# The delta-rule recurrence of a two-layer encoder on whole 128x128 tiles, with its loads spread out and its mixes in pairs

## The chip, the cores and the metric

The kernel runs on one core of one Trainium2 chip. A core has TensorE (PE in the profile, with PEld for its loads of weights), VectorE (DVE), ScalarE (ACT), GpSimd (POOL) and SyncE (SP), which here issues the DMAs. The metric is the device time of one execution in microseconds; before the change it is 2475.38 us, the median of 3 runs (2474.15 to 2476.15).

## The reference, cut to what matters

A trunk of two layers on a stream of 256 frames by 2048 channels, in float32. The first layer is an RWKV-7 time mixing with an MLP behind it; the second is an attention with forget gates and an MLP. The change touches the first layer's time mixing:

```
h  = rms_norm(x) ; prev = h shifted by one frame
xs = h + (prev - h) * x_mix[n]              # six mixes: r, k, v, w, a, g
r, k, v = xs[0..2] @ w_rkv[0..2]            # 2048 x 2048 each
decay, a, g from small two-step products of xs[3..5]
# per head (32 heads of 64), frame by frame, state S (64 x 64):
S_t = S_{t-1} diag(decay_t) + (S_{t-1} a_t) b_t^T + v_t k_t^T ;  y_t = S_t r_t
out = (group_norm(y) + bonus) * g @ w_o
```

## The kernel before

**Layout.** The 2048 channels are 16 slices of 128 partitions; a slice holds two heads of 64 channels, head 0 on partitions 0 to 63 and head 1 on 64 to 127 (`HA`, `HB`). A unit `u` is two slices, so four heads; there are 8 units. Frames are cut into 4 chunks of 64 (`NCH`). Inside a chunk the recurrence is solved with matrices: the lower-triangular system of a chunk is inverted (`inv`), then a chain over the 4 chunks carries the state (`rec`).

**Big products.** The weights stay in DRAM. `load_split` (L193 to 208) loads a raw piece `wr`, ACT casts it to a rounded fp32r copy `wh` (L203) and DVE takes the rest `wl` (L205). A few casts go to DVE (every `share["h"]`-th) and a few rests to POOL (every `share["l"]`-th). Each product is then three: wh with the high and the low part of the moving operand, wl with the high part (L211 to 213; L767 to 769 for v).

**Streams and plans.** The first layer is written as generators, one per piece of work, each yielding after a small step: `h` (norm and shifted difference), `mk`/`mr`/`mv` (the mixes for k, r, v, split into the operands opB, opA, opB), `lw`/`la`/`lg` (first small products), `gk`/`gr`/`gv` (a group of 512 columns of the big products), `gate`, `prep`, `inv`, `rec`, and `wo` (12 of the 16 slices of the output projection). `play` gives every stream a begin and an end out of a table (`PLAN_A`, then `PLAN_B`), spaces its steps evenly between them and issues the steps of all streams in the order of these numbers; the tables were written by hand or by a search, and `AFTER` says which stream must be done before another begins. The order on an engine can depart from it a little: the framework puts ready work ahead of work that waits.

**The mixes.** `h_d` (L511) makes one slice of h on DVE (L512) and its shifted difference on POOL (L513). `mix` (L521) makes one slice of xs, on DVE in one instruction (L525); `mix_steps` splits it (ACT cast L367, DVE subtraction L368), a step per slice of 128x256.

**A unit of the recurrence** (`rec_steps`, L796). Its first step issues all 13 loads of the unit on SP's queue: b, k, r, e3, k2, two pieces each of `s_at`, `s_zk` (into `RA`) and `s_v` (into `Tt`), then `s_y` into `Yf` and the gate. The second step makes `R8 = r * e3` and a diagonal `dg` on POOL. Then come three steps of 64x64 products (`pairs` twice, into `L2`; `bs`). The chain has, for each chunk c, three steps on one PSUM bank `zyus`:

1. `z`: 4 products over 128 rows and 64 columns (`halves`, L869: both heads' [a; zk] with the stacked [state; v] in `Tt`); POOL makes `sw`, the decayed state; DVE copies `zt` (128x128).
2. 4 products of `R8` with the state (L883) and 4 of the inverse `Yf` with `zt` (L887), all 64x64; ACT copies the two heads' results into `Tt` (`ua`, `ub`, 64x128 each).
3. 4 products for the next state (`sp`, not in the last chunk) and 4 for the output (`yp`), both over 128 rows and 64 columns (L869); DVE adds `sw` and `sp` into the next `Tt` (two of 64x128, L897) and copies `yt`.

So a chunk has 20 products (16 in the last) on halves or quarters of TensorE's array, with the head as the place of the half. After the chain come the statistics, 32 small 64x64 products that turn y back and add the bonus, and the split into opA. Each step's instructions go to their engines' queues in order.

Of the kernel before, what the change touches and what calls it, by code (L numbers as in the profile page):

```python
# [10 lines left out]
F32 = mybir.dt.float32  # L11
# [42 lines left out]
def shape_constants():  # L54
# [40 lines left out]
PLAN_A = {  # L95
# [6 lines left out]
}  # L102
PLAN_B = {
# [15 lines left out]
def trunk_kernel(ctx: ExitStack, tc: tile.TileContext, xin, vecs, bfv, c32, c16, w_rkv, w1, w2, a1, a2, g1, g2,  # L119
# [48 lines left out]
    def vcol(n, k):  # L168
        i = VIX[n] * KT + k
        return vec[:, i:i + 1]  # L170
# [195 lines left out]
    def split(src, oh, ol, gp=False):  # L366
        nc.scalar.copy(oh, src)  # L367
        (G if gp else V).tensor_tensor(ol, src, oh.bitcast(F32), op=ALU.subtract)  # L368
# [139 lines left out]
    def on(n):  # L508
        return lambda k: k % MIX[n][0] < MIX[n][1]

    def h_d(k):  # L511
        V.scalar_tensor_tensor(hT[:, k, 1:], xT[:, k, :], vcol("mix0", k), rs, op0=ALU.mult, op1=ALU.mult)  # L512
        (V if on("h")(k) else G).tensor_tensor(dT[:, k, :], hT[:, k, 0:T], hT[:, k, 1:], op=ALU.subtract)  # L513

    def h_steps():
        for k in range(KT):
            h_d(k)
            mixed["h"] = k + 1
            yield

    def mix(n, k, fast):  # L521
        assert k < mixed["h"]
        xs = pp.tile([P, T], F32, tag="xs", name="xs", bufs=3)
        if fast:
            V.scalar_tensor_tensor(xs, dT[:, k, :], vcol(f"xm{n}", k), hT[:, k, 1:], op0=ALU.mult, op1=ALU.add)  # L525
# [3 lines left out]
        return xs  # L529

    def mix_steps(n, oh, ol, fast):
        for k in range(KT):
            split(mix(n, k, fast(k)), oh[:, k, :], ol[:, k, :], ENG["mixl"] == "G")
            mixed[n] = k + 1
            yield

    def lora_in(n, w, rank, nk, fast, done):

        nm = (rank + P - 1) // P
        ps = side("lps").rearrange("p (m t) -> p m t", m=2)  # L540
        for k0 in range(0, KT, nk):
            raw = wraw.tile([P, nk, rank], F32, tag="wr", name="wr")
            dma(raw, w[k0 * P:(k0 + nk) * P, :].rearrange("(k p) n -> p k n", p=P))
            for kk in range(nk):
                k = k0 + kk
                xs = mix(n, k, fast(k))
                for m in range(nm):
                    c0, c1 = m * P, min(rank, (m + 1) * P)
                    mm(ps[0:c1 - c0, m, :], raw[:, kk, c0:c1], xs, start=k == 0 and m == 0, stop=k == KT - 1,
                       skip_group_check=True)  # L550
                yield
        done(ps)
# [123 lines left out]
    def inv_steps(u):  # L676
# [4 lines left out]
        def t16(tag, bufs=2):  # L681
            return ip.tile([P, 8, CH], F16, tag=tag, name=tag, bufs=bufs)
# [34 lines left out]
        bh = t16("bh")  # L717
# [77 lines left out]

    def rec_steps(u):  # L796
# [3 lines left out]
        RA = half[:, 0:1024].rearrange("p (h q c n) -> p h q c n", q=2, c=NCH, h=2)  # L800
        R8, dg = (half[:, o:o + 512].rearrange("p (c t) -> p c t", t=CH) for o in (1024, 1536))
# [7 lines left out]
        Yf = rp.tile([P, 2, NCH, CH], F32, tag="yf", name="yf", bufs=2)  # L809
# [6 lines left out]
        b8, k8 = c8(ld("b", s_b)), c8(ld("k", s_k))  # L816
        r, e3, k2 = ld("r", s_r), ld("e3", s_e3), ld("k2", s_k2)
        for h in range(2):
            own, other = H[h], H[1 - h]
            ldma(RA[own, h].rearrange("p q c n -> p (q c n)"), s_at[u, own])  # L820
            ldma(RA[other, h].rearrange("p q c n -> p (q c n)"), s_zk[u, other])

            ldma(Tt[other, h].rearrange("p c q n -> p (c q n)"), s_v[u, other])
        ldma(fl(Yf), s_y[u])
        gt = ld("gt", s_g)
        for h in range(2):
            G.memset(Tt[H[h], h, 0], 0.0)
        yield
        tt("ra", R8, c8(r), c8(e3), ALU.mult)
# [6 lines left out]
        def pairs(rhs, x, y):  # L836
            ga, gb = c64(x), c64(y)
            for c in range(8):
                quad(ga[HA, c, :], b8[HA, c, :], rhs[HA, c, :])
                quad(gb[HB, c, :], b8[HB, c, :], rhs[HB, c, :])  # L840
                quad(ga[HB, c, :], k8[HA, c, :], rhs[HA, c, :])
                quad(gb[HA, c, :], k8[HB, c, :], rhs[HB, c, :])
            return ga, gb
        ga, gb = pairs(R8, "g2a", "g2b")
# [4 lines left out]
        ga, gb = pairs(dg, "bta", "btb")  # L849
# [12 lines left out]

        yt = rp.tile([P, 2, NCH, CH], F32, tag="yt", name="yt", bufs=1)

        def halves(dst, lhs, start):

            for q in range(2):
                for h in range(2):
                    mm(dst[H[h], q, :], lhs(q, h), Tt[:, h, c, q, :], start=start and q == 0, stop=True,  # L869
                       skip_group_check=True)  # L870
        for c in range(NCH):
            zt = rp.tile([P, 2, CH], F32, tag="zt", name="zt", bufs=2)
            bank = side("zyus").rearrange("p (x q n) -> p x q n", x=4, q=2)
            zp, yp, up, sp = (bank[:, i] for i in range(4))
            halves(zp, lambda q, h: RA[:, h, q, c, :], True)
            if c < NCH - 1:
                sw = rp.tile([P, 2, 2, CH], F32, tag="sw", name="sw", bufs=1)
                tt("sw", sw, Tt[:, :, c], WC[:, p0:p0 + 2, c][:, None, :, None].to_broadcast([P, 2, 2, CH]), ALU.mult)
            cp("zt", zt, zp)
            yield  # L880
            for q in range(2):
                for h in range(2):
                    mm(yp[H[h], q, :], R8[H[h], 4 * q + c, :], Tt[H[h], h, c, q, :], start=False, stop=True,  # L883
                       skip_group_check=True)
            for q in range(2):
                for h in range(2):
                    mm(up[H[h], q, :], Yf[H[h], q, c, :], zt[H[h], q, :], start=False, stop=True,  # L887
                       skip_group_check=True)
            cp("ua", Tt[HA, 0, c], up[HA])
            cp("ub", Tt[HB, 1, c], up[HB])  # L890
            yield
            if c < NCH - 1:
                halves(sp, lambda q, h: L2[:, q, c, 192 * h:192 * h + CH], False)
            halves(yp, lambda q, h: L2[:, q, c, 64 + 64 * h:128 + 64 * h], False)
            if c < NCH - 1:
                for h, hs in enumerate((HA, HB)):
                    V.tensor_tensor(Tt[hs, h, c + 1], sp[hs], sw[hs, h], op=ALU.add)  # L897
            cp("yt", yt[:, :, c, :], yp)
            yield
# [17 lines left out]
        for c in range(8):  # L917
            for h, i in ((0, C("ident")[HA, 0:64]), (1, C("ident")[HB, 64:128])):
                quad(yp[H[h], c, :], y3[H[h], c, :], i)
                quad(vp[H[h], c, :], Tt[H[1 - h], h, c % NCH, c // NCH, :], db[H[1 - h], c, :])  # L920
# [9 lines left out]
    REC = 21  # L930
# [284 lines left out]
```

## Time and profile before

| | |
|---|---|
| median of 3 runs | 2475.38 us |
| the profiled execution: its time, its span | 2474.56 us, 2472.8 us |
| plan A (norm, mixes, k and r products, set-up) | 0 to about 275 us |
| plan B (inverse, v product, recurrence, most of the output projection) | about 275 to 612 us |
| rest of the output projection, MLP | 612 to 1340 us |
| shared keys and values, attention | 1340 to about 1747 us |
| MLP, final norm | to 2473 us |
| granted TensorE clock, mean | 0.992 |

How to read the lines that follow. A group by line has the engine, the operation, the tiles (out<-in), the shapes (partitions x elements) and the count, then busy us, the mean ns of one, and the idle time of its engine just before with what ended it. A shape such as 128*64 is the part of TensorE's array in use (rows*columns). An f32 product is two records, each with a load of weights (PEld) and a matmul (PE); an fp32r product is one. Matmuls are pipelined and their lengths overlap, so what a matmul costs is read from start to start. In rows of waits the numbers are us in total, times, longest.

### The profile page before, as it was taken

What the parts mean: (1) busy time and instruction counts of PE and PEld (TensorE: products, weight loads), DVE (VectorE), ACT (ScalarE), POOL (GpSimd) and SP (SyncE); (2) the same over time, 40 slices, a digit from 0 to 9 for tenths busy, and PEclk for the clock granted to TensorE, in tenths of its full rate; (3) what the DMA queues carried; (4) which work ended last, traced back from release to release, by engine and by line L of the source; (5) the groups of instructions that cost most, each with busy time, mean ns of one, the idle gap of its engine ahead of it and who ended that gap; (6) DMA issues with size and microseconds to landing.
All of it is one profiled execution on the core that took longest, in us unless ns stands there. A gap on an engine that the chain in (4) does not pass through costs nothing.

```text
span 2472.8 us, 45748 instructions
## 1 busy us (share of the span) xinstructions
PE 2429.4 (98%) x18336; PEld 2087.4 (84%) x18336; DVE 1513.6 (61%) x2201; ACT 1235.7 (50%) x1969; POOL 243.8 (10%) x241
## 2 busy tenths in 40 slices
PE   8999999999999999999999999999999999999998
PEld 6999877689888888888888888888888888888886
DVE  8986666765854455554557565787654555555554
ACT  3766444454654453453455544565454543443543
POOL 2000112221300010000011000111010000000001
PEclk9999999999999999999999999999999999999999
DMA  5777765564766666666665656545656666666653
GB/s 166 229 248 246 261 196 172 185 189 147 230 190 190 194 187 195 190 187 194 191 184 179 189 178 194 170 158 176 201 182 196 190 188 195 190 189 195 189 186 125
DMA packets 276565, 472.56 MB, mean 191 GB/s; under 512 B 23280, under 2 KB 70656, under 8 KB 276352
## 3 DMA queue, kind: packets, MB, share of 16 engines
q1 hardware_dynamic: 276352, 469.64, 61.2%
q8 instruction: 143, 2.34, 0.4%
q14 instruction: 70, 0.57, 0.1%
HBM read 445.44 MB, written 24.13 MB: 190 GB/s over the span
## 4 chain that ended last, share of the span: by engine, by line
PE 91%; DVE 4%; issue 2%; DMA 1%; ACT 1%; POOL 0%; SPq 0%; POOLq 0%; DVEq 0%; ACTq 0%
PE mmw L253 21%; PE mmw L257 11%; PE mmd L390 9%; PE mmd L389 9%; PE mmd L391 9%; PE mmn L271 5%; PE mm L211 3%; PE mm L212 3%; PE mm L213 3%; PE mmn L275 2%; PE mmv L767 1%; PE i L693 1%; PE mmv L768 1%; PE mmv L769 1%; PE zyus L869 1%
## 5 line engine op out<-in xcount | busy, mean ns | idle before, releaser
L205 DVE TENSOR_TENSOR wl<-wr,wh 128x1024 fp32r<-128x1024 f32 (+1 forms) x1001 | 964.1, 974 | 769.2 <-ACT wh L203 682.8
L203 ACT CAST wh<-wr 128x512 fp32r<-128x512 f32 (+1 forms) x1010 | 839.4, 837 | 976.8 <-PE mmd L390 345.0
L253 PE MATMUL mmw<-opB,wh 128*128 128x512 f32 x1280 | 321.2, 393 | 0.0
L253 PEld LDWEIGHTS mmw<-opB,wh 128*128 128x128 f32 x1280 | 230.4, 189 | 41.7 <-ACT nln L351 0.3
L253 PE MATMUL mmw<-opA,wh 128*128 128x512 f32 x1024 | 256.7, 393 | 0.0
L253 PEld LDWEIGHTS mmw<-opA,wh 128*128 128x128 f32 x1024 | 184.4, 189 | 33.3 <-ACT nln L351 0.3
L389 PE MATMUL mmd<-wh,opB 128*128 128x512 f32 x512 | 199.7, 390 | 0.0
L389 PE MATMUL mmd<-wh,opA 128*128 128x512 f32 x512 | 199.7, 390 | 0.0
L390 PE MATMUL mmd<-wh,opA 128*128 128x512 f32 x512 | 199.3, 389 | 0.0
L391 PE MATMUL mmd<-wl,opA 128*128 128x512 f32 x512 | 199.3, 389 | 0.0
L391 PE MATMUL mmd<-wl,opB 128*128 128x512 f32 x512 | 199.3, 389 | 0.0
L390 PE MATMUL mmd<-wh,opB 128*128 128x512 f32 x512 | 199.3, 389 | 0.0
L419 POOL TENSOR_TENSOR ms<-mt 128x512 f32<-128x512 f32 x64 | 78.5, 1239 | 1157.7 <-ACT mt L417 1157.7
L257 PEld LDWEIGHTS mmw<-opB,wl 128*128 128x128 f32 x1280 | 174.5, 190 | 14.9 <-DVE wl L205 2.6
L257 PE MATMUL mmw<-opB,wl 128*128 128x256 f32 x1280 | 178.7, 283 | 1.8 <-DVE wl L205 1.8
L211 PE MATMUL mm<-opA,wh 128*128 128x256 f32 x512 | 150.5, 294 | 0.0
L257 PEld LDWEIGHTS mmw<-opA,wl 128*128 128x128 f32 x1024 | 139.8, 190 | 10.0
L212 PE MATMUL mm<-opA,wh 128*128 128x256 f32 x512 | 145.5, 284 | 0.0
L213 PE MATMUL mm<-opA,wl 128*128 128x256 f32 x512 | 145.1, 283 | 0.0
L257 PE MATMUL mmw<-opA,wl 128*128 128x256 f32 x1024 | 142.8, 282 | 0.0
L391 PEld LDWEIGHTS mmd<-wl,opB 128*128 128x128 f32 x512 | 96.1, 188 | 20.0
L391 PEld LDWEIGHTS mmd<-wl,opA 128*128 128x128 f32 x512 | 96.1, 188 | 20.0
(293 smaller groups left out, 3833.5 us busy)
## 6 DMA issues: line engine op xcount, KB each, us to landing
wr<-in_mlp_w_up_dram SPq DMA_DIRECT2D x256, 512.0 KB, 3.8
wr<-in_mlp_w_down_dram SPq DMA_DIRECT2D x256, 512.0 KB, 3.7
wr<-in_w_rkv_dram SPq DMA_DIRECT2D x96, 512.0 KB, 5.0
wr<-in_w_kvf_dram SPq DMA_DIRECT2D x64, 512.0 KB, 3.7
wr<-in_w_o_dram SPq DMA_DIRECT2D x32, 512.0 KB, 4.6
wr<-in_fox_w_q_dram SPq DMA_DIRECT2D x32, 512.0 KB, 3.5
wr<-in_fox_w_o_dram SPq DMA_DIRECT2D x32, 512.0 KB, 3.7
wr<-in_g_dram SPq DMA_DIRECT2D x8, 512.0 KB, 4.7
```

The lines of the kernel that those rows point to most:

```text
L203: nc.scalar.copy(h, raw[:, k:k + per, :])
L205: (G if share["l"] and c % share["l"] == 0 else V).tensor_tensor(lo, raw[:, k:k + per, :], h.bitcast(F32), op=ALU.subtract)
L211: mm(ps, wh, xh, start=first and bank_first, stop=False, skip_group_check=True)
L212: mm(ps, wh, xl, start=False, stop=False, skip_group_check=True)
L213: mm(ps, wl, xh, start=False, stop=last, skip_group_check=True)
L253: mm(ps[m], h[:, m * P:(m + 1) * P], x[:, k].rearrange("p h t -> p (h t)"), start=k == 0, stop=False, skip_group_check=True)
L257: mm(ps[m][:, 0:T], lo[:, m * P:(m + 1) * P], x[:, k, 0, :], start=False, stop=k == KT - 1, skip_group_check=True)
L271: mm(ps[m], hl[i][0][:, m * P:(m + 1) * P], x[:, k0 + i].rearrange("p h t -> p (h t)"), start=k0 + i == 0, stop=False, skip_group_check=True)
L389: mm(ps[i], b[:, k, 0, t], h, start=k == 0, stop=False)
L390: mm(ps[i], b[:, k, 1, t], h, start=False, stop=False)
L391: mm(ps[i], b[:, k, 0, t], lo, start=False, stop=k == KT - 1)
L419: G.tensor_tensor(s, t, t, op=ALU.mult)
```

## The change

- **The chain on whole tiles.** `RA` becomes, for each head h, slice and chunk, a 128x128 matrix: on the other head's rows zk in head h's [a; zk] columns and zeros beside it, on head h's rows a in one half of the columns and `r * e3` in the other. So one product `z1` gives z and the state's part of y together: 4 products of 128 rows and 128 columns with 64 moving columns per chunk, where 4 (z) and 4 (R8) stood. The zeros are set by POOL for the first two units only, since the two buffers are used in turn.
- `YBD` holds the inverses of the two heads of a slice as a block diagonal (again with zeros set once): 2 products for a chunk instead of 4.
- The last products take 128 columns of `L2` at a time (state and output together, `s2`): 4 for a chunk instead of 8, in the last chunk as well, where the state half is not used. A chunk has 10 products in all.
- **Evacuation.** `zt` is taken in two copies on DVE (`za`, `zb`, 64x128 each) and the whole of `z1` in a third (`zy`, 128x256); `sw` is made by two POOL instructions of 64x128; y is two DVE additions (64x128 each) of `s2` and `zy` where one copy stood. The halves of y's heads are now swapped, which the small products at the end undo.
- `ra` is two POOL instructions of 64 partitions by 512 elements instead of one of 128 by 512.
- **Loads.** They are spread: b, r, e3 in the first step; k and the two `s_at` pieces in the second (with the memsets); k2 and the two `s_zk` pieces in the third; the two `s_v` pieces with the first `pairs`; `s_y` as two pieces with the second; the gate ahead of the chain. The at, zk and y pieces now fall into runs of 64 elements (256 bytes) in SBUF. A unit has 22 steps instead of 21.
- **Mixes by pairs.** `h` makes two slices and then one difference of 128x512, on DVE instead of POOL; `mix_steps` makes two slices of xs and splits them with one ACT cast and one DVE subtraction of 128x512. `xs` has 2 buffers of two slices instead of 3 of one.
- **Order and shares.** Many entries of both plans are changed; the casts given to DVE in plan B go from every 8th to every 10th; `bh` has one buffer instead of two.

```diff
 MIX = {
-    "h": (1, 0), "k": (4, 4), "r": (2, 2), "v": (3, 3), "w": (1, 1), "a": (1, 1), "g": (3, 3),
+    "h": (1, 1), "k": (1, 1), "r": (2, 2), "v": (1, 1), "w": (1, 1), "a": (1, 1), "g": (3, 3),
 }
-SHARE_B = {"h": 8, "l": 5}
+SHARE_B = {"h": 10, "l": 5}
...
     def h_steps():
+        for k in range(0, KT, 2):
+            for j in (k, k + 1):
+                V.scalar_tensor_tensor(hT[:, j, 1:], xT[:, j, :], vcol("mix0", j), rs, op0=ALU.mult, op1=ALU.mult)
+                if j == k:
+                    yield
+            (V if on("h")(k // 2) else G).tensor_tensor(dT[:, k:k + 2, :], hT[:, k:k + 2, 0:T], hT[:, k:k + 2, 1:],
+                                                        op=ALU.subtract)
+            mixed["h"] = k + 2
+            yield
...
     def mix_steps(n, oh, ol, fast):
+        for k in range(0, KT, 2):
+            xs = pp.tile([P, 2, T], F32, tag="xs", name="xs", bufs=2)
+            mix(n, k, fast(k), xs[:, 0, :])
+            yield
+            mix(n, k + 1, fast(k + 1), xs[:, 1, :])
+            split(xs, oh[:, k:k + 2, :], ol[:, k:k + 2, :], ENG["mixl"] == "G")
+            mixed[n] = k + 2
             yield
...
+    YBD = rp.tile([P, 2, 8, P], F32, name="YBD", bufs=1)
...
+        RA = half.rearrange("p (h c n) -> p h c n", h=2, c=8)
+        YB = YBD[:, u % 2]
+        LO, HI = slice(0, CH), slice(CH, P)
+        SA, SR = (LO, HI), (HI, LO)
...
+        b8, r, e3 = c8(ld("b", s_b)), ld("r", s_r), ld("e3", s_e3)
+        yield
+        k8 = c8(ld("k", s_k))
         for h in range(2):
+            ldma(RA[H[h], h, :, SA[h]], sat[H[h]])
+            if u < 2:
+                G.memset(RA[H[1 - h], h, :, SR[h]], 0.0)
+                G.memset(YB[H[h], :, SR[h]], 0.0)
+            G.memset(Tt[H[h], h, 0], 0.0)
+        yield
+        k2 = ld("k2", s_k2)
         for h in range(2):
+            ldma(RA[H[1 - h], h, :, SA[h]], szk[H[1 - h]])
+            tt("ra", RA[H[h], h, :, SR[h]], c8(r)[H[h]], c8(e3)[H[h]], ALU.mult)
...
+        HQ = [(h, q) for h in range(2) for q in range(2)]
+        for c in range(NCH):
+            zt = rp.tile([P, 2, CH], F32, tag="zt", name="zt", bufs=2)
+            bank = side("zyus")
+            z1, up, s2 = (bank[:, a:b].rearrange("p (h q n) -> p h q n", q=2, n=CH)
+                          for a, b in ((0, 256), (256, 384), (256, 512)))
+            for h, q in HQ:
+                mm(z1[:, h, q, :], RA[:, h, NCH * q + c, :], Tt[:, h, c, q, :], start=True, stop=True,
+                   skip_group_check=True)
+            if c < NCH - 1:
+                sw = rp.tile([P, 2, CH], F32, tag="sw", name="sw", bufs=1)
+                for h in range(2):
+                    tt("sw", sw[H[h]], Tt[H[h], h, c], WC[H[h], p0:p0 + 2, c:c + 1].to_broadcast([CH, 2, CH]), ALU.mult)
+            cp("za", zt[HA], z1[HA, 0])
+            cp("zb", zt[HB], z1[HB, 1])
+            zy = rp.tile([P, 2, 2, CH], F32, tag="zy", name="zy", bufs=2)
+            cp("zy", zy, z1)
+            yield
             for q in range(2):
+                mm(up[:, 0, q, :], YB[:, NCH * q + c, :], zt[:, q, :], start=True, stop=True, skip_group_check=True)
+            cp("ua", Tt[HA, 0, c], up[HA, 0])
+            cp("ub", Tt[HB, 1, c], up[HB, 0])
+            yield
+            for h, q in HQ:
+                mm(s2[:, h, q, :], L2[:, q, c, h * P:h * P + P], Tt[:, h, c, q, :], start=True, stop=True,
+                   skip_group_check=True)
+            if c < NCH - 1:
                 for h in range(2):
+                    V.tensor_tensor(Tt[H[h], h, c + 1], s2[H[h], h], sw[H[h]], op=ALU.add)
+            for h in range(2):
+                V.tensor_tensor(yt[H[1 - h], :, c, :], s2[H[1 - h], h], zy[H[1 - h], h], op=ALU.add)
             yield
...
-    REC = 21
+    REC = 22
```

More of the change, by code (lines that the diff above doesn't have):

```diff
@@ L509, in on, with mix @@
         return lambda k: k % MIX[n][0] < MIX[n][1]
-    def h_d(k):
-        V.scalar_tensor_tensor(hT[:, k, 1:], xT[:, k, :], vcol("mix0", k), rs, op0=ALU.mult, op1=ALU.mult)
-        (V if on("h")(k) else G).tensor_tensor(dT[:, k, :], hT[:, k, 0:T], hT[:, k, 1:], op=ALU.subtract)
     def h_steps():
-        for k in range(KT):
-            h_d(k)
-            mixed["h"] = k + 1
+        for k in range(0, KT, 2):
[6 more added lines that the diff above has]
+            mixed["h"] = k + 2
             yield
-    def mix(n, k, fast):
+    def mix(n, k, fast, xs):
         assert k < mixed["h"]
-        xs = pp.tile([P, T], F32, tag="xs", name="xs", bufs=3)
         if fast:
@@ L545, in lora_in @@
                 k = k0 + kk
-                xs = mix(n, k, fast(k))
+                if kk % 2 == 0:
+                    pair = pp.tile([P, 2, T], F32, tag="xs", name="xs", bufs=2)
+                xs = pair[:, kk % 2, :]
+                mix(n, k, fast(k), xs)
                 for m in range(nm):
@@ L716, in inv_steps @@
         sdma(s_zk[u], zk.rearrange("p c t -> p (c t)"))
-        bh = t16("bh")
+        bh = t16("bh", 1)
         cp("bh", bh, cn)
@@ L815, in ld @@
             return t
-        b8, k8 = c8(ld("b", s_b)), c8(ld("k", s_k))
-        r, e3, k2 = ld("r", s_r), ld("e3", s_e3), ld("k2", s_k2)
+        sat, szk, sy = (s[u].rearrange("p (c t) -> p c t", t=CH) for s in (s_at, s_zk, s_y))
+        b8, r, e3 = c8(ld("b", s_b)), ld("r", s_r), ld("e3", s_e3)
+        yield
+        k8 = c8(ld("k", s_k))
         for h in range(2):
[L819 to L826, printed above, removed]
+            ldma(RA[H[h], h, :, SA[h]], sat[H[h]])
+            if u < 2:
+                G.memset(RA[H[1 - h], h, :, SR[h]], 0.0)
+                G.memset(YB[H[h], :, SR[h]], 0.0)
             G.memset(Tt[H[h], h, 0], 0.0)
         yield
-        tt("ra", R8, c8(r), c8(e3), ALU.mult)
+        k2 = ld("k2", s_k2)
+        for h in range(2):
+            ldma(RA[H[1 - h], h, :, SA[h]], szk[H[1 - h]])
+            tt("ra", RA[H[h], h, :, SR[h]], c8(r)[H[h]], c8(e3)[H[h]], ALU.mult)
         tt("dg", dg, bcast(C("ids"), 8), WC[:, p0:p0 + 2, :].rearrange("p q c -> p (q c)")[:, :, None]
@@ L834, in rec_steps, with pairs @@
         L8 = c8(L2)
-        def pairs(rhs, x, y):
+        def pairs(ra, rb, x, y):
             ga, gb = c64(x), c64(y)
             for c in range(8):
[L839 to L842, printed above, removed]
+                quad(ga[HA, c, :], b8[HA, c, :], ra[HA, c, :])
+                quad(gb[HB, c, :], b8[HB, c, :], rb[HB, c, :])
+                quad(ga[HB, c, :], k8[HA, c, :], ra[HA, c, :])
+                quad(gb[HA, c, :], k8[HB, c, :], rb[HB, c, :])
             return ga, gb
-        ga, gb = pairs(R8, "g2a", "g2b")
+        ga, gb = pairs(*(RA[:, h, :, SR[h]] for h in range(2)), "g2a", "g2b")
+        for h in range(2):
+            ldma(Tt[H[1 - h], h].rearrange("p c q n -> p (c q n)"), s_v[u, H[1 - h]])
         V.tensor_tensor(L8[:, :, 64:128], ga, bcast(C("mle"), 8), op=ALU.mult)
@@ L847, in rec_steps @@
         yield
-        ga, gb = pairs(dg, "bta", "btb")
+        ga, gb = pairs(dg, dg, "bta", "btb")
+        for h in range(2):
+            ldma(YB[H[h], :, SA[h]], sy[H[h]])
         cp("bt", L8[:, :, 0:64], ga)
@@ L861, in rec_steps @@
         yield
+        gt = ld("gt", s_g)
         yt = rp.tile([P, 2, NCH, CH], F32, tag="yt", name="yt", bufs=1)
[L865 to L870, printed above, removed]
+        HQ = [(h, q) for h in range(2) for q in range(2)]
         for c in range(NCH):
             zt = rp.tile([P, 2, CH], F32, tag="zt", name="zt", bufs=2)
-            bank = side("zyus").rearrange("p (x q n) -> p x q n", x=4, q=2)
-            zp, yp, up, sp = (bank[:, i] for i in range(4))
-            halves(zp, lambda q, h: RA[:, h, q, c, :], True)
-            if c < NCH - 1:
-                sw = rp.tile([P, 2, 2, CH], F32, tag="sw", name="sw", bufs=1)
-                tt("sw", sw, Tt[:, :, c], WC[:, p0:p0 + 2, c][:, None, :, None].to_broadcast([P, 2, 2, CH]), ALU.mult)
-            cp("zt", zt, zp)
+            bank = side("zyus")
[4 more added lines that the diff above has]
+                   skip_group_check=True)
+            if c < NCH - 1:
+                sw = rp.tile([P, 2, CH], F32, tag="sw", name="sw", bufs=1)
+                for h in range(2):
+                    tt("sw", sw[H[h]], Tt[H[h], h, c], WC[H[h], p0:p0 + 2, c:c + 1].to_broadcast([CH, 2, CH]), ALU.mult)
[3 more added lines that the diff above has]
+            cp("zy", zy, z1)
@@ L880, in rec_steps @@
             yield
             for q in range(2):
-                for h in range(2):
[L883 to L889, printed above, removed]
@@ new lines, in rec_steps @@
+            cp("ua", Tt[HA, 0, c], up[HA, 0])
[5 more added lines that the diff above has]
+            if c < NCH - 1:
+                for h in range(2):
+                    V.tensor_tensor(Tt[H[h], h, c + 1], s2[H[h], h], sw[H[h]], op=ALU.add)
+            for h in range(2):
+                V.tensor_tensor(yt[H[1 - h], :, c, :], s2[H[1 - h], h], zy[H[1 - h], h], op=ALU.add)
@@ L917, in rec_steps @@
         for c in range(8):
-            for h, i in ((0, C("ident")[HA, 0:64]), (1, C("ident")[HB, 64:128])):
-                quad(yp[H[h], c, :], y3[H[h], c, :], i)
+            for h, i in ((0, C("ident")[HB, 64:128]), (1, C("ident")[HA, 0:64])):
+                quad(yp[H[h], c, :], y3[H[1 - h], c, :], i)
                 quad(vp[H[h], c, :], Tt[H[1 - h], h, c % NCH, c // NCH, :], db[H[1 - h], c, :])
```

17 lines of the change are left out of this document (1 added, 16 removed), and 27 rows, old and new, of tables (ENG, PLAN_A, PLAN_B).

## The prediction

> **What bounds the kernel now.** I read the page first (engine shares, then the chain that ended last), then the busy time of each engine in the stage that the change rewrites.
>
> ```profile
> span 2472.8 us, 45748 instructions
> PE 2429.4 (98%) x18336; PEld 2087.4 (84%) x18336; DVE 1513.6 (61%) x2201; ACT 1235.7 (50%) x1969; POOL 243.8 (10%) x241
> PE 91%; DVE 4%; issue 2%; DMA 1%; ACT 1%; POOL 0%; SPq 0%; POOLq 0%; DVEq 0%; ACTq 0%
> ```
>
> TensorE is busy for 98% of the span and is 91% of the chain. No other engine is near that. The recurrence (plan B) runs from about 275 to 612 us. The table by stage has, per engine, busy us and instructions, then the granted clock, the DMA share and GB/s; the second row is the front of plan A.
>
> ```profile
> 275.00:612.00 337.00, 321.10 (x6561) 264.81 (x6560) 218.03 (x405) 151.46 (x312) 75.03 (x82) 0.96 0.61 190
> 14.00:60.00 46.00, 40.20 (x242) 32.80 (x242) 45.22 (x92) 20.16 (x43) 12.63 (x16) 0.93 0.42 130
> ```
>
> In the recurrence TensorE is busy for 321 of 337 us, DVE for 218, ACT for 151. So a microsecond of TensorE time added there is nearly a microsecond of the end. In the front, DVE is the full one (45.22 of 46).
>
> **How TensorE spends the recurrence.** Durations of matmuls overlap, so I price by start-to-start times in the timeline (start us, length, engine, line).
>
> ```profile
> 412.93 0.39 PE L768 MATMUL mmv<-wh,opB 128*128 128x512 f32 x1
> 413.16 0.40 PE L769 MATMUL mmv<-wl,opB 128*128 128x512 f32 x1
> 413.49 0.45 PE L869 MATMUL zyus<-Tt,xT 128*64 128x64 f32 x8
> 413.87 0.50 PE L767 MATMUL mmv<-wh,opB 128*128 128x512 f32 x1
> 414.21 0.39 PE L768 MATMUL mmv<-wh,opB 128*128 128x512 f32 x1
> ```
> ```profile
> 415.82 0.39 PE L769 MATMUL mmv<-wl,opB 128*128 128x512 f32 x1
> 416.14 0.31 PEld L883 LDWEIGHTS zyus<-Tt,xT 64*64 64x64 f32 x8 [0.35 <-DVE wl L205]
> 416.37 0.32 PEld L887 LDWEIGHTS zyus<-zt,yf 64*64 64x64 f32 x8
> 416.75 0.19 PEld L767 LDWEIGHTS mmv<-wh,opB 128*128 128x128 f32 x1
> 416.86 0.19 PEld L768 LDWEIGHTS mmv<-wh,opB 128*128 128x128 f32 x1
> ```
> ```profile
> 1564.64 0.31 PEld L1064 LDWEIGHTS sp<-kT,qT 128*128 128x128 f32 x2
> ```
>
> Three prices come out.
>
> (a) Half-array records. An f32 product leaves two records. The eight records of L883 start at 416.14 and L887's follow at 416.37: 0.23 us for four products, because two 64-column tiles run side by side. That is 0.029 us a record, 0.058 us a side-by-side pair.
>
> (b) Whole-array weight loads. At 416.75 and 416.86 two 128x128 loads start 0.11 us apart. Wide matmuls start 0.23 apart (412.93, 413.16), so the second load did not wait for a matmul: 0.11 is what a load occupies. L1064's two loads of f32 weights take 0.31 together where one takes 0.19, so 0.12 apart.
>
> (c) A visit to the tiled modes. From L769 at 413.16 to L768 at 414.21 is 1.05 us. Two wide starts and eight records (0.23 each) would be 0.69, so going in and out costs 0.36 us. A change from one tiled mode to another (128x64 to 64x64) is cheaper:
>
> ```profile
> 418.35 0.69 PE L869 MATMUL zyus<-Tt,L 128*64 128x64 f32 x16
> 418.96 1.15 PE L807 MATMUL yp<-k,yt 64*64 64x64 f32 x32
> ```
>
> 0.61 us for 16 records that are worth 0.46: 0.15 us. Between the first and the last tiled matmul of the stage (below) I count 108 visits and 60 changes inside visits; 31 visits hold nothing but chain products, the other 77 hold products of the inverse or of a unit's set-up and end too.
>
> ```profile
> 285.27 0.27 PE L706 MATMUL g1b<-AT,Bi 64*64 64x64 f32 x2
> ...
> 608.72 0.22 PE L807 MATMUL vp<-db,Tt 64*64 64x64 f32 x1
> ```
>
> Visits cost about 108 x 0.36 + 60 x 0.15 = 48 us of the stage. That is what whole tiles attack.
>
> **The change, part by part.**
>
> *The chain's products.* Counts from the groups by line in this stage:
>
> ```profile
> L869 PE MATMUL zyus<-Tt,L 128*64 128x64 f32 x448 | 22.2, 236 | 3.3 <-issue 1.9 <-ACT Tt L177 1.4
> L869 PE MATMUL zyus<-Tt,xT 128*64 128x64 f32 x256 | 15.8, 240 | 1.6 <-ACT X L177 0.7 <-DVE X L723 0.6
> L883 PE MATMUL zyus<-Tt,xT 64*64 64x64 f32 x256 | 14.9, 232 | 0.2 <-DVE zt L179 0.2
> L887 PE MATMUL zyus<-zt,yf 64*64 64x64 f32 x256 | 14.0, 221 | 0.0
> ```
>
> Before: 1216 records x 0.029 = 35 us. After: in each of 8 x 4 chunk steps 4 products with RA, 2 with YB and 4 with L2 (in the last chunk too, where half the L2 result is thrown away): 320 products, 640 records, each with a 128-column load. The trace has no such record with 64 moving columns. Bounds: 0.058 us if only the streaming counts (that of a pair, 37 us in all), 0.12 us if the load does (77 us). I take 0.11 us, since loads of that shape are seen 0.11 apart under whatever streams: 70 us. **Term: +35 us (+2 to +42).** Half as many instructions, but each loads twice the columns, alone instead of side by side.
>
> The Trainium skill, "TensorE: Matmul & The Clock Gate", section "Back-to-back issue gap", gives N/2.4 + 2.5 ns per matmul: an estimate of 29 ns a pass, 58 for the two passes of an f32 record, by which this term would be about +2 us. The same section warns that the formula leaves out the loading of weights, and the 0.11 us between two loads at 416.75 speaks for the warning; it is the first rival below.
>
> *Mode changes.* The 31 chain-only visits and the inside changes go (31 x 0.36 + 60 x 0.15 = 20 us). But chain products now cut some of the 77 remaining visits in two. At the most each tiled step is a visit: 7 units of the inverse x 15 and 8 recurrence units x 4 make 137. I take 95, nearer to 77 because most inverse steps already stand alone: 95 x 0.36 = 34 us against 48. **Term: -14 us (-20 to +1).**
>
> *Waits and the clock.* The stage's granted clock of 0.96 is 13 us of lost clock, most of it in three spells:
>
> ```profile
> 326.50:336.50 10.00, 6.94 (x218) 5.78 (x214) 4.04 (x6) 3.01 (x6) 1.04 (x1) 0.80 0.67 228
> 379.00:387.00 8.00, 8.00 (x116) 5.83 (x109) 4.72 (x8) 2.16 (x4) 0.91 (x3) 0.57 0.74 218
> 471.00:479.50 8.50, 6.77 (x114) 4.99 (x113) 5.50 (x10) 2.54 (x6) 2.29 (x4) 0.60 0.52 167
> ```
>
> Two of them have TensorE idle for 1.7 to 3 us. More TensorE work in the same steps and a new order will fill some gaps: I count one spell in three. **Term: -4 us (-13 to 0).** The Trainium skill (same page, "Part 1: The HAM clock gate") has the clock halved after an idle window of some 3.4 us; the spells here follow idle time, as it says, and by it a dense stage would win all 13 us.
>
> *Work of the other engines.*
>
> ```profile
> L897 DVE TENSOR_TENSOR Tt<-zyus,sw 64x128 f32<-64x128 f32 x48 | 13.8, 287 | 14.1 <-PE zyus L869 9.3 <-ACT X L177 2.7 <-ACT L L177 1.4
> L179 DVE COPY zt<-zyus 128x128 f32<-128x128 f32 x32 | 9.1, 288 | 9.2 <-PE zyus L869 9.2
> L179 DVE COPY yt<-zyus 128x128 f32<-128x128 f32 x32 | 9.0, 289 | 7.5 <-PE zyus L869 6.4 <-ACT wh L203 0.5
> L182 POOL TENSOR_TENSOR sw<-Tt,WC 128x256 f32<-128x256 f32 x24 | 15.2, 632 | 86.4 <-DVE Tt L897 52.1 <-DMA xT<-s_at 10.1 <-DMA Tt<-v 10.0
> L182 POOL TENSOR_TENSOR xT<-r,e 128x512 f32<-128x512 f32 x8 | 11.0, 1373 | 19.6 <-PE zyus L883 10.6 <-DMA e<-s_e 7.1 <-DMA r<-s_r 1.9
> ```
>
> DVE's chunk was one zt, one yt and two Tt: 1.15 us. It becomes za and zb (0.29 each, by width), zy of twice yt's width (0.29 to 0.58, say 0.42), two Tt and two yt additions (0.29 each): 2.14 us; 32 x 0.99 = +32 us, 250 of some 350 us. POOL's sw is halved into two (0.32 to 0.63 each) and its ra too (up to 1.37 each): up to 26 us on 75. Both hide beside TensorE; uncovered they are the third rival. zy is behind za and zb, so the U products do not wait for it, but weight splits queue behind it on DVE. Casts moved from every 8th to every 10th and the ACT copies ua, ub change nothing that is late.
>
> *Loads.* A unit's loads (13, now 14) leave SP's queue over six steps instead of one, so weight loads queue less behind their buffer waits:
>
> ```profile
> SPq L195 <- DVE wl L205: 70.5, 34, 12.1
> SPq L814 <- POOL k L182: 14.9, 4, 5.3
> ```
>
> The weight queue mostly waits for its own slots (L195, 70.5 us), four loads ahead of use, so I count nothing; the at, zk and y loads fall into 256-byte pieces, hidden by a DMA share of 0.61. If one of them lands late, its unit's next step waits, and another stream's step is there to run.
>
> *Mixes by pairs (plan A).*
>
> ```profile
> L513 POOL TENSOR_TENSOR xT<-hT 128x256 f32<-128x256 f32 x16 | 12.6, 794 | 28.4 <-DVE hT L512 22.4 <-issue 5.9
> L525 DVE SCALAR_TENSOR_TENSOR xs<-xT,vec,hT 128x256 f32<-128x256 f32 x42 | 22.2, 561 | 0.0
> L368 DVE TENSOR_TENSOR opB<-xs,opB 128x256 fp32r<-128x256 f32 x16 | 8.3, 520 | 0.1
> ```
> ```profile
> L525 DVE SCALAR_TENSOR_TENSOR xs<-xT,vec,hT 128x256 f32<-128x256 f32 x41 | 18.3, 481 | 0.2 <-PE lps L549 0.2
> L182 DVE TENSOR_TENSOR hsl<-ksq,hsh 128x512 fp32r<-128x512 f32 x5 | 3.4, 688 | 1.2 <-ACT hsh L177 1.2
> ```
>
> The front's DVE gains 8 differences of 0.69 that POOL did (+5.5 us), saves 8.3 - 8 x 0.69 = 2.8 on the splits, and gets back 42 x 0.08 = 3.4 if POOL beside it is what stretches L525 from 481 (after 60 us) to 561. The first product waits about a microsecond longer for its pair; later splits save DVE some 2 us. **Term: -1 us (-5 to +4).**
>
> **Sum.** The profiled execution took 2474.6 us (span 2472.8 and 1.8 around it), 0.8 under the median. 2474.6 + 35 - 14 - 4 - 1 = 2490.6: **2491 us**, slower by 0.6%.
>
> **Rivals.**
>
> 1. *Whole tiles stream as fast as a pair (faster).* At 0.058 us a record the first term is +2: 2474.6 + 2 - 14 - 4 - 1 = 2458 us. The other terms give back 19 us, so it decides at (35 + 19) / 640 = 0.084 us a record: below that the change wins. For it: loads can be fetched ahead. Against: loads themselves stand 0.11 apart. Chance 0.12.
>
> 2. *The order heals the rest.* Only 77 visits (-20), all lost clock back (-13), the front at its best (-5): 2474.6 + 35 - 38 = 2472 us, no change or a little faster. For it: the plans are rewritten throughout and tiled steps can be laid together. Against: all three at once. Chance 0.16, of it 0.09 faster by over 0.2%.
>
> 3. *The longer step becomes the wait.* A chunk step gets 0.65 us more TensorE time ahead of za, another 0.29 for a second copy, and DVE's queue is longer by 0.99. If 1 us of each of the 32 is exposed: 2491 + 32 = 2523 us. For it: POOL's sw and the Tt copies already wait on each other. Against: two units overlap and wide work fills in. Chance 0.08.
>
> **How the numbers follow.** The forecast has 0.64, of it 0.03 within 0.2% (5 us, about what a measurement of this kernel can tell from no change). Faster 0.12 + 0.09 = 0.21; same 0.07 + 0.03 = 0.10; slower 0.61 + 0.08 = 0.69. The range, 2464 to 2514 us, takes in the second rival, the first term's upper bound with the other terms at my values (2498) and their ends to within 8 us; it leaves out the first rival and the third. The likeliest case's own range is 2479 to 2512.
>
> **What would show it.** Right: in the changed kernel records of 128x128 with 64 moving columns about 0.11 us apart, 640 of them; visits fewer than 108, nearer 95, and no 128x64 mode; DVE's busy time in the recurrence 30 us higher; the stage some 17 us longer and everything after 612 us the same. Wrong: such records 0.06 us apart; a stage no longer than 337 us; or a front that is shorter by more than 5 us.

## The result

| | median of runs, us | ratio to before |
|---|---|---|
| before | 2475.77 (2474.15 to 2478.70, 4 runs) | |
| after | 2517.49 (2498.06 to 2527.37, 4 runs) | 1.016 (1.0132 to 1.0187) |
| after, once more on another chip | 2521.72 (2519.97 to 2524.03, 4 runs) | 1.0186 (1.017 to 1.0201) |

The change makes the kernel slower by 42 to 48 us. The sign was forecast; the size lies outside the range (2464 to 2514). All comparisons below are of undisturbed executions; the one slow execution (the profiled one of run 10, 6095.88 us) is left out. The profiled execution of after took 2510.59 us at a clock of 0.990. Its page, the span, the engines and the chain:

```profile
span 2508.8 us, 44647 instructions
...
PE 2463.0 (98%) x17760; PEld 2132.5 (85%) x17760; DVE 1538.5 (61%) x2279; ACT 1235.9 (49%) x1947; POOL 252.8 (10%) x265
...
PE 93%; DVE 3%; issue 2%; DMA 1%; ACT 1%; SPq 0%; POOL 0%; POOLq 0%; DVEq 0%; ACTq 0%
```

TensorE bounds it as before, with 576 fewer matmuls and 34 us more busy time. Where the time came from is read off the first product of the MLP, which ends the recurrence's stage; in the row of a tile the two times are the starts of the first and the last instruction of the window. Before, then after:

```profile
L253 PE MATMUL mmw<-opB,wh x112: 388/392/398, 643.8 to 684.0; 128*128 128x512 f32 x112
```
```profile
L254 PE MATMUL mmw<-opB,wh x16: 388/391/397, 678.9 to 683.3; 128*128 128x512 f32 x16
```

643.8 us became 678.9: 35.1 us later, and the span grew by 36.0. The first product with v starts at 286.4 us before and at 285.3 after, so plan A gave a microsecond at most, everything behind the stage kept its length within a microsecond, and the loss is in the recurrence. The table by stage of after (columns as before; the last two rows are one stretch at half clock and the one behind it):

```profile
275.00:612.00 337.00, 322.27 (x5643) 274.50 (x5642) 224.67 (x450) 137.83 (x284) 92.95 (x115) 0.95 0.59 177
14.00:60.00 46.00, 37.59 (x232) 32.07 (x233) 44.82 (x96) 15.08 (x28) 0.00 (x0) 0.93 0.43 132
473.70:494.20 20.50, 20.50 (x249) 16.75 (x238) 9.94 (x27) 5.06 (x12) 4.99 (x7) 0.50 0.26 89
494.20:514.00 19.80, 19.78 (x289) 16.09 (x288) 13.24 (x29) 9.26 (x22) 7.09 (x8) 1.00 0.58 161
```

In the same 337 us TensorE is as full as before (322 against 321) and gets through 918 fewer matmuls. The chain's own groups, and the start-to-start time of its records at full clock:

```profile
L910 PE MATMUL zyus<-Tt,L 128*128 128x64 f32 x256 | 36.6, 285 | 0.6 <-ACT Tt L178 0.6
L893 PE MATMUL zyus<-Tt,xT 128*128 128x64 f32 x256 | 35.7, 284 | 0.1
L905 PE MATMUL zyus<-zt,YBD 128*128 128x64 f32 x128 | 20.4, 284 | 1.9 <-DVE zy L180 1.7
```
```profile
495.02 1.10 PE L893 MATMUL zyus<-Tt,xT 128*128 128x64 f32 x8
495.94 0.48 PE L774 MATMUL mmv<-wh,opB 128*128 128x512 f32 x1
```

640 records; eight of them take 0.92 us from start to start, 0.115 each (the median between two is 0.112). Now the same eight inside the half-clock stretch:

```profile
478.14 1.97 PE L893 MATMUL zyus<-Tt,xT 128*128 128x64 f32 x8
479.90 1.06 PE L905 MATMUL zyus<-zt,YBD 128*128 128x64 f32 x4
480.72 0.77 PE L776 MATMUL mmv<-wl,opB 128*128 128x512 f32 x1
```

1.76 us, 0.22 a record. The clock stays at 0.50 for 20.5 us while TensorE is busy 20.50 of 20.50 us. In the stage of before the three half-clock spells last 10.2, 6.8 and 6.8 us (24); here 3.4, 6.8, 20.5 and 3.4 (34).

A start-to-start account of the stage, from its first tiled product to its last (my sums over the timeline; the changes of mode are priced over the steady spacing of each kind of product, and shift by some 3 us with how that is averaged): chain records 35 -> 69 us; changes of mode 276 (39.0 us) -> 204 (33.0 us); what is left beyond the steady spacing of each kind of product 20.1 -> 28.4 us. +34 - 6 + 8 = +36, against 35.1 seen.

### The profile page after: what moved, and what is told of

Same layout as the page of the kernel before. It is cut to its first block, busy times and chain, and to the rows that moved or that the text cites. A ratio compares the mean times of both kernels' runs of the same rounds, so it can differ in the third digit from the quotient of the medians.

```text
span 2508.8 us, 44647 instructions
## 1 busy us (share of the span) xinstructions
PE 2463.0 (98%) x17760; PEld 2132.5 (85%) x17760; DVE 1538.5 (61%) x2279; ACT 1235.9 (49%) x1947; POOL 252.8 (10%) x265
## 4 chain that ended last, share of the span: by engine, by line
PE 93%; DVE 3%; issue 2%; DMA 1%; ACT 1%; SPq 0%; POOL 0%; POOLq 0%; DVEq 0%; ACTq 0%
PE mmw L254 21%; PE mmw L258 11%; PE mmd L392 9%; PE mmd L391 9%; PE mmd L390 9%; PE mmn L272 5%; PE mm L212 3%; PE mm L214 3%; PE mm L213 3%; PE mmn L276 2%; PE i L700 2%; PE mmv L774 1%; PE mmv L776 1%; PE mmv L775 1%; PE zyus L910 1%
```

## The experiments

Theories at the start. **W**: the whole tile is dear by itself (a record of 0.112 us that loads 128 columns and streams 64). **D**: the chain's longer DVE work (0.99 us a chunk) is the cost. **M**: the rest of the change (plans, loads, POOL, mixes) costs. Later **H**: the clock, halved while half-empty products (64 columns behind a load of 128) run. The expectations below, as recorded, also use O (the new order and the longer copies), C (the clock), L (the 256-byte loads, in runs 5 and 6 together with POOL's halved instructions), P (POOL's work) and B (the second PSUM bank). Each kernel was timed against before on the same chip; distances to after are across chips, except for runs 5 to 7, which share run 8's.

**1. Whole tiles back to half tiles**, all else as after; every chain product in two halves of the columns:

```diff
-                mm(z1[:, h, q, :], RA[:, h, NCH * q + c, :], Tt[:, h, c, q, :], ...)
+                for s in H:
+                    mm(z1[s, h, q, :], RA[:, h, NCH * q + c, s], Tt[:, h, c, q, :], ...)
```
(the same for `up` and `s2`)

> The changed kernel, with each whole-tile product of the chain issued as two products of 128 rows by 64 columns (same operands, loads, copies and plans). Theory W (the 128-column load of weights sets 0.11 us a record): 1280 records at 0.029 us instead of 640 at 0.11 take 34 us off, and the chain's visits to a tiled mode come back at 5 to 12 us, so 2485 to 2495 us where the changed kernel has 2517. Theory O (the new order and the longer copies make the wait): no better than 2510. Theory C (the halved clock makes all of what was not forecast): about 2495, with the same share of slow clock as the changed kernel.

Measured 2496.01 us (2494.24 to 2497.93), ratio 1.0086 (1.0071 to 1.0101). Its chain:

```profile
L914 PE MATMUL zyus<-Tt,L 128*64 128x64 f32 x512 | 24.4, 231 | 3.3 <-ACT Tt L178 3.3
L894 PE MATMUL zyus<-Tt,xT 128*64 128x64 f32 x512 | 23.3, 237 | 0.1
L907 PE MATMUL zyus<-zt,YBD 128*64 128x64 f32 x256 | 15.3, 237 | 2.7 <-DVE zy L180 1.4 <-issue 1.1
```

Twice the records in 63 us of busy time where 93 stood. Some 21 to 26 us of the loss go with the whole tile, although 120 mode changes return (324 in all, 48.1 us against 33.0). About 20 us stay that are not the whole tile.

**2. The old chain, everything else as after** (plans, spread loads, mixes, casts): `R8`, `Yf`, the 20 products and the single copies of before.

POOL's `sw` and `ra` in one piece and the long loads of at, zk and y go back with it.

> The changed kernel with the chain of before (R8, 64x64 and 128x64 products, its copies), but the new plans, the spread loads and the mixes by pairs. Theory W: near the kernel before, 2468 to 2482 us. Theory O: the new order costs by itself, 2495 us or more.

Measured 2475.28 us, 1.0001 (0.9991 to 1.001). The whole loss belongs to the chain's rewrite and what goes with it; of M the plans, the spreading of the loads and the mixes are out, POOL's halved instructions and the 256-byte loads are left to runs 9 and 10. The stage:

```profile
275.00:612.00 337.00, 320.32 (x6499) 264.10 (x6498) 215.74 (x400) 151.17 (x311) 77.66 (x85) 0.98 0.61 190
```

**3. Mixes by pairs and plan A alone**, on before (`h_steps`, `mix_steps`, their table and `PLAN_A`).

> The kernel before with the mixes by pairs and the new plan A alone. All theories: the recurrence begins as early as before, so 2475 us within 4.

Measured 2476.12 us, 1.0008 (0.9998 to 1.0017): nothing.

**4. The z1 products twice** (the second writes the same result):

```diff
+                for _ in range(2):
-                mm(z1[:, h, q, :], RA[:, h, NCH * q + c, :], ...)
+                    mm(z1[:, h, q, :], RA[:, h, NCH * q + c, :], ...)
```

> The changed kernel with the first products of each chunk (z1) issued twice: 128 products, 256 records more, same result. Theory W: 256 x 0.11 = 28 us more than the changed kernel, 2540 to 2550 us. If a whole-tile record cost what a pair of halves does (0.058): 15 us more. Theory O (TensorE has slack and the copies are the wait): under 8 us more.

Measured 2542.94 us (2537.93 to 2546.91), 1.0268 (1.0249 to 1.0288): 21 to 25 us above after for 256 more records, 0.08 to 0.10 us each. They are on the path at nearly their full 0.11 (0.106 at equal clock, by the line of run 8); W is confirmed as a price.

**5. Half tiles with compact evacuation**: z and y in shared columns of PSUM, y added up there, so DVE copies once for zt and once for yt as before.

```diff
-            zy = rp.tile([P, 2, 2, CH], F32, tag="zy", name="zy", bufs=2)
-            cp("zy", zy, z1)
...
+            halves(zp, lambda q, h: RA[:, h, NCH * q + c, SA[h]], tq, 0, True)
+            halves(yp, lambda q, h: RA[:, h, NCH * q + c, SR[h]], tq, 1, False)
+            cp("za", zt, zp)
```

> The halves run again, but with z and y of both heads in the same PSUM columns and y summed up in PSUM, so that DVE takes them as the kernel before does (one zt, one yt, two Tt per chunk); loads, POOL's work and plans stay those of the changed kernel. Theory D (the second half of the loss is DVE's 32 us of extra copies and the steps that they lengthen): 2475 to 2482 us. Theory L (it is the 256-byte loads and POOL's halved instructions): still 2490 to 2497.

Measured 2493.13 us (2485.31 to 2496.91), 1.0065 (1.0042 to 1.0089). Only 3 us below run 1, inside its own scatter: taking the extra copies off the half tiles gave next to nothing, against D. It keeps 326 mode changes (45.2 us before 646 us).

**6. DVE's copies as a dose on the old chain**: two zt copies, a 128x256 copy that nothing reads, yt in two copies.

> The old chain in the new plans with the changed kernel's DVE work laid on it: zt in two copies, a copy of 128x256 that nobody reads, y in two copies; TensorE, loads and POOL as in the old chain. Theory D: 2485 to 2497 us where the old chain had 2475. Theory L: 2475 to 2480.

```profile
L179 DVE COPY yt<-zyus 64x128 f32<-64x128 f32 x64 | 18.4, 288 | 2.0 <-PE zyus L876 0.4 <-PE vp L813 0.3
L179 DVE COPY zt<-zyus 64x128 f32<-64x128 f32 x64 | 18.3, 287 | 6.5 <-PE zyus L876 5.6
L179 DVE COPY zy<-zyus 128x256 f32<-128x256 f32 x32 | 13.6, 424 | 0.6
```

32 us more DVE work, and 2486.33 us (2481.63 to 2489.49), 1.0044 (1.0028 to 1.0061): 11 us above run 2. So D is right in kind, at a third of its work. It is not a plain wait of TensorE: between the first product with v and the first of the MLP TensorE is idle for 21.3 us, in run 2 for 19.1, while that stretch is 6 us longer. Part of it may go by way of the order: with DVE fuller the framework lays TensorE's instructions out otherwise, with 316 mode changes (45.0 us before 646 us) where run 2 has 296 (40.3). That is argued and not shown: run 9 has 297 changes, which by the same kind of account also take 5 us more than those of run 2, and it lost no more than 1 us.

**7. z1 with 128 moving columns** (both slices' columns are streamed, half of the product is thrown away; one more PSUM bank):

```diff
+            zb4 = side("zyz").rearrange("p (h q r n) -> p h q r n", h=2, q=2, r=2)
-                mm(z1[:, h, q, :], RA[:, h, NCH * q + c, :], Tt[:, h, c, q, :], ...)
+                mm(zb4[:, h, q], RA[:, h, NCH * q + c, :], Tt[:, h, c], ...)
```

> The changed kernel with 128 moving columns instead of 64 in each of the four z1 products (both slices' columns are streamed, one half of each result is thrown away; one PSUM bank more per chunk). Theory W (a whole-tile record lasts as long as its load of 128 columns): the records stay 0.11 us apart and the time stays within 8 us of the changed kernel, or is lower if more streaming keeps the clock up. If streaming set the pace: 256 records x 0.05 = 14 us more, and records at 0.16.

Measured 2501.68 us (2497.57 to 2506.48), 1.0111 (1.0091 to 1.013), 16 to 20 us *faster* than after with more streamed. Its stage and its chain:

```profile
275.00:612.00 337.00, 321.56 (x5751) 278.00 (x5749) 228.88 (x469) 142.98 (x295) 95.20 (x119) 0.99 0.62 182
```
```profile
L893 PE MATMUL zyz<-Tt,xT 128*128 128x128 f32 x256 | 36.2, 285 | 0.1
L910 PE MATMUL zyus<-Tt,L 128*128 128x64 f32 x256 | 34.1, 275 | 0.6 <-ACT Tt L178 0.6
```

A record of 128 columns has the mean length of one of 64 (285 and 284 ns), and the median from start to start is 0.112 us for both; so at 64 columns the streaming does not set the pace; the load of the weights, which is the same in both, is what is left. And the clock is 0.99 in the stage, with two half-clock spells of 3.4 us each. This brought up H.

**8. After once more, on the chip of run 7.**

> The changed kernel again, for its spread and its clock. Theory C (the part that differs from run to run is TensorE's halved clock in the recurrence): time falls with the granted clock along one line, about 0.7 us per us of lost clock; runs at the clock of before (0.993) lie near 2502, so that the clock makes 15 of the 42 us. Rival (the spread has another cause): no such line.

Measured 2521.72 us. Two of its half-clock stretches:

```profile
438.80:459.30 20.50, 20.50 (x226) 18.07 (x224) 8.60 (x21) 3.18 (x9) 5.99 (x7) 0.50 0.36 100
476.30:513.80 37.50, 37.50 (x414) 30.56 (x410) 17.77 (x43) 8.83 (x20) 8.78 (x10) 0.50 0.34 104
```

In all 68 us at half clock in the recurrence, TensorE busy in every microsecond of these two. The eight runs of after, by clock, are 2498.06 (0.996), 2510.59 (0.990), 2519.97, 2521.57 and 2521.86 (0.984), 2524.40 (0.983), 2524.03 (0.982) and 2527.37 us (0.979). A line through them is 2492.2 + 0.71 us for each microsecond of lost clock ((1 - clock) x time), correlation 0.99. At before's mean clock (0.9935, 16 us lost) it gives 2504: some 16 us of the loss are clock.

**9. POOL's halved instructions on the old chain** (`sw` and `ra` a head at a time).

> The old chain in the new plans, with POOL's work split as in the changed kernel: ra in two instructions of 64 partitions, sw in two of 64x128; TensorE, DVE and loads as in the old chain (2475). Theory P (POOL's 20 us more in its queue hold up the state and the weight splits behind it): 2481 to 2488 us. Otherwise within 4 us of 2475.

Measured 2476.02 us, 1.0006 (0.9997 to 1.0015): nothing.

**10. The 256-byte loads and the shared `YBD` tile on the old chain.**

> The old chain in the new plans, with at, zk and y loaded into the changed kernel's places (runs of 256 bytes, y in two loads into the shared tile); all products and copies as in the old chain. Theory L (the small pieces and the shared tile make units wait for their loads): 2481 to 2490 us. Otherwise within 4 us of 2475.

Measured 2477.3 us, 1.001 (1.0 to 1.0019): about 2 us (0 to 5).

**11. Runs 6, 9 and 10 together.**

> The old chain with all three loads of work laid on it: DVE's extra copies, POOL's halved instructions, the 256-byte loads. If these three are what is left between the old chain (2475) and the changed kernel on half-array products (2493 to 2496): 2490 to 2497 us. If the zero-padded products over 128 rows, their changes of mode and their clock make a part: 2484 to 2489.

Measured 2488.01 us (2485.31 to 2492.78), 1.0049 (1.0035 to 1.0063). The three doses add up to 13 us, most of it DVE's. To the half tiles of run 1 (2496) 8 us are left (6 at equal clock, below); that they are the zero-padded products over 128 rows and their mode changes (324 against 316) is argued, not shown.

**12. z1 in a bank of its own, but 64 columns**: run 7 without the wider stream.

```diff
-                mm(zb4[:, h, q], RA[:, h, NCH * q + c, :], Tt[:, h, c], ...)
+                mm(zb4[:, h, q, q], RA[:, h, NCH * q + c, :], Tt[:, h, c, q], ...)
```

> The z1 products in a PSUM bank of their own, as in the run with 128 moving columns, but with the changed kernel's 64. Theory C (more streaming per load kept the clock up): as slow as the changed kernel, 2512 to 2525 us, with a granted clock of 0.980 to 0.988. Rival B (the second bank, or the order that goes with it, made that run faster): 2498 to 2506 us at 0.993.

Measured 2506.96 us (2498.09 to 2511.23), 1.0116 (1.009 to 1.0141), clock 0.987 to 0.995, 48 us at half clock in its profile. The longest spell of that profile:

```profile
442.50:463.00 20.50, 20.50 (x234) 17.78 (x236) 9.14 (x22) 4.43 (x10) 6.14 (x8) 0.50 0.48 135
```

The run lies between after and run 7; its runs stand 2 to 6 us below after's line, those of run 7 2 to 4. So at equal clock the wider stream gives nothing more than the bank does, and what parts the two is the clock, by 0.003 in the mean, which is no more than the scatter of four runs each. The profiles part them better. The four of kernels with whole tiles at 64 columns throughout (after, runs 4, 8 and 12) each have a half-clock spell of 20.5 us or longer in the recurrence; none of the other ten (before, runs 1 to 3, 5 to 7, 9, 11 and 13) has one over 10.2, and in the two with the wider stream (7 and 13) the longest are 3.4 and 6.8. So the long spells go with the half-empty stream, and the bank alone does not end them. That is one profile of each kernel, and not a test of the cause.

**13. z1 and the inverse's products with 128 columns.**

```diff
-                mm(up[:, 0, q, :], YB[:, NCH * q + c, :], zt[:, q, :], ...)
+                mm(uw[:, q], YB[:, NCH * q + c, :], zt, ...)
```
(on run 7; half of these products too is thrown away)

> The run with 128 moving columns for z1, and now for the two products with the inverse as well. Theory C: the clock stays at 0.993 or above and the time is that of 128 columns for z1 alone (2502) within 6 us, although 64 columns more stream in 128 records. If streaming cost time: 128 x 0.05 = 6 us more.

Measured 2502.96 us (2499.26 to 2504.41), 1.0109 (1.0094 to 1.0124): as run 7, no further gain. Its expectation held: the clock was 0.993 to 0.996, and the added columns cost nothing.

## Why the prediction was right or wrong

**Right: the bound and the sign.** TensorE sets the end, the loss is in the recurrence, and what follows keeps its length.

**Right: the whole-tile record.** 0.11 us was taken, 0.112 was measured; the term of +35 came out as +34, and run 4 shows these records on the path. The first rival, 0.058 us as a pair streams, is out. The estimate from the Trainium skill ("TensorE: Matmul & The Clock Gate", "Back-to-back issue gap") is out with it at 64 columns, 58 ns against 112: run 7 doubles N at no cost, where that formula grows with N.

**Mis-sized: mode changes.** -14 was forecast with 95 visits at 0.36 us. There were 102 visits, and over the whole stage those of before cost 39.0 us, not the 48 that one visit's 0.36 and the inside changes' 0.15 made of them; 39.0 -> 33.0 is -6.

**Failed: "Waits and the clock", -4 us (-13 to 0).** The sign is wrong. More TensorE work of this kind did not lift the clock: after spends 34 and 68 us of the stage at half clock in its two profiles, before 24. By the line of run 8 the median execution loses about 16 us more to the clock than before does (one of the eight, at 0.996, loses less, and still takes 2498.06). The prediction read the spells of before as a result of idle time. The Trainium skill (same page, "Part 1: The HAM clock gate") says that a busy window of some 3.4 us restores the clock. The spells are indeed multiples of 3.4 us (6.8, 20.5, 37.5), but 20.5 us of full "busy" did not end one: the measurement decides, and busy in the profile is not what the gate counts.

For how a spell begins, the reading was sound. In the recurrence of the 14 profiles (all but run 10's) the clock changes on a grid of 3.41 us in each. Of the 74 stretches of that grid (275 to 650 us) at full clock with TensorE busy for at most 70%, 43 were followed by one at half clock; of the 1353 others, 15. What was not foreseen is what ends it. Of the 97 stretches at half clock with TensorE busy throughout, 42 of the 64 with at most 1536 columns of wide products (those that stream 256 or 512 columns; 1536 is three of 512) were followed by another at half clock, but 3 of the 33 with more. Of these 42, 35 are in the four profiles with whole tiles at 64 columns. So work that fills TensorE's time and streams little goes with a clock that stays low. What exactly the gate counts is not shown; the half-empty stream is the best candidate.

**Failed: "Both hide beside TensorE".** For POOL it holds (run 9). For DVE it does not: 32 us of added copies cost 11 to 13 (runs 6 and 11). The extra work is there as counted:

```profile
L180 DVE COPY zt<-zyus 64x128 f32<-64x128 f32 x64 | 18.4, 288 | 14.1 <-PE zyus L893 13.5
L916 DVE TENSOR_TENSOR yt<-zyus,zy 64x128 f32<-64x128 f32 x64 | 18.4, 287 | 8.2 <-PE vp L820 3.4 <-PE zyus L910 2.9 <-ACT X L178 0.9
L914 DVE TENSOR_TENSOR Tt<-zyus,sw 64x128 f32<-64x128 f32 x48 | 13.9, 289 | 21.4 <-PE zyus L910 17.4 <-ACT Y L178 2.5 <-PE mm L213 0.7
L180 DVE COPY zy<-zyus 128x256 f32<-128x256 f32 x32 | 13.6, 424 | 0.5
```

64.3 us where 32 stood. The third rival had DVE's longer queue as a cost, at 32 us with a chance of 0.08; by the dose of run 6 it is about a third of that. Its mechanism, an exposed wait, is not what the traces show: between the first product with v and the first of the MLP TensorE is idle for 15.9 us before and 15.6 after, and the dose of run 6 added 2.2. The prediction did not look for another way, such as the order of TensorE's instructions; which one it is stays open, and run 5, which takes the copies off the half tiles, got only 3 us back.

**Right: loads, POOL and mixes.** Each within 2.3 us of before in the median (runs 2, 3, 9, 10). In the front DVE's xs instruction fell from 561 to 477 ns with POOL idle beside it (0.00 in the table), as read:

```profile
L526 DVE SCALAR_TENSOR_TENSOR xs<-xT,vec,hT 128x256 f32<-128x256 f32 x46 | 20.5, 477 | 0.7 <-PE lps L556 0.6
```

It moved no end.

**The sum that the runs give.** With the clock taken out by the line of run 8 (each run's distance from it, mean over a kernel's runs), run 2 stands 28 us below after, run 6 20, run 11 16, run 1 10, and after itself at 0. So, from 2475: DVE's copies 8 at equal clock, with POOL and the loads 11 (run 11); to the half tiles 6 (run 1, the padded products, argued); to the whole tiles 10; the clock 16. 11 + 6 + 10 + 16 = 43, and 2518 lies between the two medians of after. The shares of the first two depend on the order in which the parts are laid on: run 5 alone would put DVE's copies at 3. In the prediction the last three had +35 - 14 - 4 = +17 to cover, and the first nothing. The range failed because the clock had no upper end above nothing and the DVE work one only in a rival that was left out.

**Open.** What the clock goes by; how DVE's copies reach the end; how the 6 to 8 us between runs 11 and 1 come about; and whether the chain would do better under the plans of before, which was not tried. No version beat before; run 2 equals it.

## What to carry to other kernels

A block diagonal halves the instructions, but where the load of the weights sets the pace it pays for its zeros: compare the loads' start-to-start times, alone and side by side, with the mode changes that go. In a stage with a full TensorE, work on another engine is not hidden because TensorE is busy: 32 us of copies cost 11 here, with TensorE idle only 2 us longer. Put a price above zero on both, and on the clock.

## What was not expected of the hardware

- TensorE can be busy for 20.5 and 37.5 us on end at a clock of 0.50; a record of 128 rows, 128 columns and 64 moving columns then takes 0.22 us, where it takes 0.112.
- In the recurrence, a 3.41 us stretch at half clock with TensorE busy throughout was followed by another in 42 of 64 cases with at most 1536 columns of wide products in it, and in 3 of 33 with more.
- Streaming 128 columns in place of 64 behind such a load cost no time, and its runs had a clock of 0.991 to 0.996, where the runs of after on that chip had 0.982 to 0.984.
- One kernel's runs spread over 29 us (2498.06 to 2527.37), and the lost clock explains nearly all of it, at 0.71 us of time per microsecond lost.
